# Weight tiles staged a chunk ahead at the changes of operand, and the bias table written in the first stage from GpSimd's queue

## The chip, the cores and the metric

The kernel runs on one core of a Trainium2 chip. What counts is the time of one execution on the device in microseconds. The kernel before took 2283.38, 2283.22 and 2278.28 us in three runs; the median is 2283.22 us.

## What is computed

One decoder layer for a prompt of 2048 tokens and for 8 single-token samples, with width 1024. All tokens share the weights, so the kernel works on 2056 columns of tokens:

```python
h = x * (1 + scale) + shift                       # scale, shift, gate from silu(c) @ w_ada + b_ada
u_s, z_s, q, k, v, z_a, g_s, g_a = split(h @ w_in)
b_s = (GLU(gelu(S5(u_s))) * silu(z_s)) @ w_branch_s
b_a = (attention(q, k, v) * silu(z_a)) @ w_branch_a
m   = sigmoid(g_s) * b_s + sigmoid(g_a) * b_a
x   = LayerNorm(alpha * x + gate * (m @ w_out))
```

The attention looks at a window of 128 keys with a bias by distance. The bias is a table of 32 buckets by 16 heads, `rel_bias`. The kernel turns it into a row of 384 numbers for each head and writes that row 128 times into a scratch tensor in device memory, `biasD` (16 heads x 128 x 384 numbers, 3 MB). Read back with a step of 383, it gives the band of biases for a block of queries. The 8 samples use the same table without the scratch tensor.

## The kernel before

**Products.** Every large matrix product goes through `split_w`, `chunk` and `products`. A weight tile of 1024 x 128 numbers is loaded into `wst` (L55, one buffer). ScalarE rounds it to `whi` (L58) and VectorE takes the rest, `wlo` (L59). An operand X lies in five chunks of tokens (512, 512, 512, 256, 264 wide), each as a high and a low part. One chunk of one job is 24 matmuls (L78): 8 slices of the contraction by three terms. `products` asks for the next job's weights after the second chunk of a job.

**Stages.** The first stage computes u_s, then two jobs for z_a with the work on gate beside them, then v (`v_proj`, L665). `v_proj` takes 17 tiles of tokens, each of 24 matmuls, copies each result from `acc` (3 buffers in PSUM) to `vt` and sends it to device memory from ScalarE's queue. `vt` shares a pool of two buffers (tag `ev`) with the results of all jobs before it, z among them. The second stage runs the state-space scan beside jobs, the third the attention beside jobs. The third begins with `attn_setup`, which writes the bias table (L895, on SyncE's queue) and computes the 8 samples' attention: scores, a softmax in `t1s`, then a transpose of `t1s` on TensorE (L940). Its jobs are `raw_job`s, which copy `acc` to `zr` on ScalarE (L586, also tag `ev`) and send it to `zsD` from ScalarE's queue (L587).

**Changes of operand.** In the fourth stage the operand changes three times, from h to the scan's output, then to the attention's output, then to the gated output. `turn` does the last two jobs of one operand chunk by chunk, and loads a chunk of the next operand into the space that each chunk leaves. It first loads a chunk (`load(0)`), then takes the second job's weights (`split_w(jobs[1][0])`), and in the last chunk, after the first of the two jobs, the weights of the job after the turn (`split_w(nxt)`). The chunks come in the order 512, 256, 512, 264, 512 columns (`ORD`).

**What sets the order.** The program is not run in the order in which the code is written. A scheduler takes the recorded instructions with their dependences and decides each engine's order, which is then fixed. Every engine works through its own list in order. SyncE (SP), ScalarE (ACT) and, for a transfer that the code puts there, GpSimd (POOL) issue transfers. Transfers from SP and ACT take their completion counters from one set of eight in turn, so a transfer is issued only when the one eight places before it is done. Transfers from GpSimd's queue have counters of their own.

Of the kernel before, what the change touches and what calls it, by code (L numbers as in the profile page):

```python
# [9 lines left out]
F32 = mybir.dt.float32  # L10
# [11 lines left out]
KT = 8  # L22
ORD = (0, 3, 1, 4, 2)
# [16 lines left out]
class Trunk:  # L40
# [5 lines left out]
        return es.enter_context(self.tc.tile_pool(name=name, bufs=bufs, reuse_waits="tile", **kw))  # L46


    def split_w(self, parts, st=None):

        nc = self.nc
        if st is None:
            st = self.wp.tile([128, KT, 128], F32, name="wst", bufs=1)
        for src, dst in parts:
            nc.sync.dma_start(dst(st), src)  # L55
        hi = self.wp.tile([128, KT, 128], F32R, name="whi")
        lo = self.wp.tile([128, KT, 128], F32R, name="wlo")
        nc.scalar.copy(hi, st)  # L58
        nc.vector.tensor_tensor(lo, st, hi, op=OP.subtract)  # L59
        return hi, lo  # L60
# [3 lines left out]

    def chunk(self, W, X, c, tick=None):

        nc = self.nc
        ps = self.gp.tile([128, 512], F32, name="acc")
        for k in range(KT):
            self.chunk_k(ps, W, X, c, k)  # L70
            if tick is not None and k in (2, 5, 7):
                tick()
        return ps

    def chunk_k(self, ps, W, X, c, k):
        (hi, lo), (xh, xl), n = W, X[c], CH[c][1]
        for i, (w, x) in enumerate(((hi, xh), (hi, xl), (lo, xh))):
            self.nc.tensor.matmul(ps[:, :n], w[:, k, :], x[:, k, :], start=(k == 0 and i == 0), stop=(k == KT - 1 and i == 2))  # L78

    def products(self, jobs, X, nxt=None, tick=None, first=ORD):  # L80

        for i, (parts, evac, begin, end) in enumerate(jobs):
            W = self.nextW if self.nextW is not None else self.split_w(parts)
            self.nextW = None
            if begin:
                begin()
            for ci, c in enumerate(ORD if i else first):
                ps = self.chunk(W, X, c, tick)
                evac(c, ps)
                if ci == 1:  # L90
                    p2 = jobs[i + 1][0] if i + 1 < len(jobs) else nxt
                    if p2 is not None:
                        self.nextW = self.split_w(p2)
            if end:
                end()

# [520 lines left out]
    def phase1(self, ues, up):  # L617
        nc, I = self.nc, self.I
        w = I["w_in"][0]
        with ExitStack() as ses:  # L620
            self.sps = self.pool(ses, "sp1", 2, PSUM)
            with ues, ExitStack() as es:
                self.prp = self.pool(es, "prep")
                side = self.ssm_prep()
                jobs = []
                for m in range(1, 8):
                    b, e, f = self.u_job(up, m)
                    if m == 1:
                        def b(b=b, e=e):
                            b()  # L630
                            e(ORD[0], self.early)
                    jobs.append((self.cols(w, U0 + m * 128), e, b, f))
                self.products(jobs, self.X, self.cols(w, ZA0), self.every(3, side), first=ORD[1:])
                for _ in side:
                    pass
            with ExitStack() as es:
                p = self.pool(es, "p1z", 2)
                side = self.gate(p)
                self.products([self.za_job(m) for m in range(2)], self.X, self.cols(w, ZA0 + 256), self.every(2, side))
                for _ in side:  # L640
                    pass
                self.v_proj(p)
        for nm, src in (("sk", "cache_swa_k"), ("sv", "cache_swa_v")):
            self.tc.keep_in_program_order(
                nc.sync.dma_start(self.O[nm][0, :, 0:127].rearrange("b w g d -> b w (g d)"),
                                  I[src][0, :, 1:128].rearrange("b w g d -> b w (g d)")))
# [233 lines left out]
        for h in range(nh):  # L880
            v.tensor_scalar(t1[:, h, kw], t1[:, h, kw], den[:, h:h + 1], None, op0=OP.mult)

    def attn_setup(self, p, pp):
        nc, I = self.nc, self.I
        oh = p.tile([32, 129], F32, name="oh")
        nc.sync.dma_start(oh, I["c_onehot"])
        rb = p.tile([32, 16], F32, name="rb")
        nc.sync.dma_start(rb, I["rel_bias"])
        pr = pp.tile([16, 129], F32, name="pt", bufs=2)
        nc.tensor.matmul(pr, rb, oh, start=True, stop=True)  # L890
        fr = p.tile([16, 384], F32, name="fr")

        nc.vector.memset(fr, NEG)
        nc.vector.tensor_scalar(fr[:, 127:256], pr, 8.0, None, op0=OP.mult)
        nc.sync.dma_start(self.biasD.rearrange("h (r l) -> h r l", l=384), fr[:, None, :].to_broadcast([16, 128, 384]))  # L895

        rr = p.tile([32, NS, 16], F32, name="rr")
        nc.vector.tensor_copy(rr, rb[:, None, :].to_broadcast([32, NS, 16]))
# [23 lines left out]
        for b in range(NS):  # L922
# [6 lines left out]
            for P in range(2):  # L929
                i = b * 2 + P  # L930
# [186 lines left out]
    def phase3(self, n2, n3, ii):  # L1117
        with ExitStack() as es:
            pp = self.pool(es, "sp3", 2, PSUM)
            with ExitStack() as es2:  # L1120
                p = self.pool(es2, "p3s")
                side = self.attn_setup(p, pp)
                self.products([self.raw_job(i) for i in range(n2, n2 + n3)], self.X, self.raw_parts(n2 + n3),
                              lambda: next(side, None))
                for _ in side:
                    pass
            with ExitStack() as es2:
                p = self.pool(es2, "p3", 2)
                side = self.attn_blocks(p, pp, ii)
                self.products([self.raw_job(i) for i in range(n2 + n3, 22)], self.X, self.raw_parts(22), lambda: next(side, None))  # L1130
                for _ in side:
                    pass

    def turn(self, jobs, X, nxt, src, where):

        new = [None] * 5

        def load(c):
            new[c] = self.load_x(c, src, where[c])

        load(0)
        W = [self.nextW, self.split_w(jobs[1][0])]
        for c in ORD:
            for i, (parts, evac, begin, end) in enumerate(jobs):
                ps = self.chunk(W[i], X, c)
                if c == 2 and i == 0:
                    self.nextW = self.split_w(nxt)
                evac(c, ps)
            if c != 2:
                load({0: 1, 1: 2, 3: 3, 4: 4}[c])  # L1150
        return new
# [53 lines left out]
    def phase4(self):  # L1205
        nc, I = self.nc, self.I
# [11 lines left out]
        X = self.turn([self.raw_job(i) for i in (22, 23)], self.X, self.cols(wg, 0), self.from_y, "BAAAA")  # L1218

        first = (0, 3, 1, 2, 4)  # L1220

        def ahead(job, first=ORD, n=6):

            seq = [(m, c) for m in range(n) for c in (ORD if m else first)]
            seq += [(m, c) for c in ORD for m in range(n, 8)]
            loaded, ready = {}, {}

            def load(i):
                if i < len(seq) and i not in loaded:
                    loaded[i] = job.load(*seq[i])  # L1230

            def prep(i):
                if i < len(seq) and i not in ready:
                    ready[i] = job.prep(*seq[i], loaded[i])

            def evac(m, c, ps):
                i = seq.index((m, c))
                load(i)
                prep(i)
                load(i + 1)  # L1240
                job.fin(m, c, ps, ready[i])
                prep(i + 1)

            return [(self.cols(job.w, m * 128), lambda c, ps, m=m: evac(m, c, ps), None, None) for m in range(8)]
# [21 lines left out]
                nc.sync.dma_start(self.ysD[m][:, o:o + n], sg[:, :n])  # L1266

        jobs = ahead(Glu(), first)
        self.products(jobs[:6], X, jobs[6][0], first=first)
        X2 = self.turn(jobs[6:], X, self.cols(wa, 0), self.from_(self.ozD), "ABAAA")  # L1270

        class BranchA:
# [14 lines left out]
                nc.sync.dma_start(self.paD[m][:, o:o + n], t[:, :n])  # L1287

        jobs = ahead(BranchA())
        self.products(jobs[:6], X2, jobs[6][0])  # L1290
        X3 = self.turn(jobs[6:], X2, self.cols(ws, 0), self.from_(self.ysD), "AABAA")

        class BranchS:
# [18 lines left out]
        jobs = ahead(BranchS(), n=8)  # L1312
# [166 lines left out]
```

## Time and profile before

| | |
|---|---|
| profiled execution | 2283.26 us, its span 2281.5 us |
| median of three runs | 2283.22 us |
| TensorE busy | 2227.6 us, 98% of the span |
| VectorE busy | 1462.5 us, 64% |
| ScalarE busy | 787.5 us, 35% |
| GpSimd busy | 342.4 us, 15% |

The span is the time between the first and the last instruction. The rest of the execution, 1.76 us, lies around it. TensorE's granted clock is shown as a share of full speed: 1.00 is 2.4 GHz and 0.50 is 1.2 GHz.

### The profile page before, as it was taken

The numbers are of one execution on the slowest core, as the hardware profiler recorded it, in microseconds if no ns is written. First come the engines' busy times: TensorE is split into PE (matmuls) and PEld (weight loads), VectorE is DVE, ScalarE is ACT, GpSimd is POOL, SyncE is SP. The second block draws the span as 40 slices with busy tenths as digits, with TensorE's granted clock in tenths as the row PEclk, the third lists the DMA queues.
The fourth block names the chain that finished last, engine by engine and source line by source line (L and its number), as shares of the span: only waits on it lengthen the run. The fifth ranks groups of instructions, "written<-read, shape, count | busy, mean of one in ns | idle before, by whom it ended". The sixth has DMA issues, their size and how long they took to land.

```text
span 2281.5 us, 35066 instructions
## 1 busy us (share of the span) xinstructions
PE 2227.6 (98%) x12571; PEld 1908.1 (84%) x12571; DVE 1462.5 (64%) x3576; ACT 787.5 (35%) x1700; POOL 342.4 (15%) x420
## 2 busy tenths in 40 slices
PE   7999999999999999999999999999979999999997
PEld 5888798888888888788888888888868888888886
DVE  4896219897888883168998888565354124124887
ACT  3411212332111111157777677573233123112100
POOL 1100001111111111000000000014541001232232
PEclk9999999999999999999999999999989999999999
DMA  9344523334434343743334343486347447667431
GB/s 298 103 141 144 181 95 105 116 113 119 126 115 116 118 120 95 141 131 111 111 113 140 113 118 107 108 195 187 107 144 229 125 126 243 185 187 224 148 111 66
DMA packets 387502, 317.98 MB, mean 139 GB/s; under 512 B 89334, under 2 KB 331406, under 8 KB 385743
## 3 DMA queue, kind: packets, MB, share of 16 engines
q1 hardware_dynamic: 349616, 260.28, 40.2%
q10 hardware_dynamic: 37712, 55.47, 7.2%
q8 instruction: 99, 1.62, 0.3%
q14 instruction: 75, 0.61, 0.1%
HBM read 195.24 MB, written 122.63 MB: 139 GB/s over the span
## 4 chain that ended last, share of the span: by engine, by line
PE 81%; DMA 8%; DVE 5%; SPq 2%; issue 2%; ACT 1%; POOL 1%; ACTq 0%; POOLq 0%; DVEq 0%
PE acc L78 59%; PE po L1413 7%; PE ps L1045 3%; PE po L1088 3%; PE pt L1072 2%; DMA z<-zsD 2%; PE acc L665 2%; DMA biasD<-fr 2%; DMA tD<-kt 1%; SPq L178 1%; PE yp L817 1%; PE yp L816 1%; PE xp L784 1%; DVE sg L1265 1%; PE tr L230 0%
## 5 line engine op out<-in xcount | busy, mean ns | idle before, releaser
L78 PE MATMUL acc<-hh,whi 128*128 128x512 f32 (+2 forms) x2000 | 713.7, 357 | 0.0
L78 PE MATMUL acc<-hl,whi 128*128 128x512 f32 (+2 forms) x2000 | 704.7, 352 | 0.0
L78 PE MATMUL acc<-hh,wlo 128*128 128x512 f32 (+2 forms) x2000 | 703.3, 352 | 0.1
L78 PEld LDWEIGHTS acc<-hh,whi 128*128 128x128 f32 x2000 | 377.7, 189 | 49.0 <-issue 1.9
L78 PEld LDWEIGHTS acc<-hl,whi 128*128 128x128 f32 x2000 | 378.0, 189 | 48.4 <-issue 1.9
L78 PEld LDWEIGHTS acc<-hh,wlo 128*128 128x128 f32 x2000 | 377.5, 189 | 48.1 <-issue 1.0
L78 PE MATMUL acc<-xh,whi 128*128 128x512 f32 (+2 forms) x960 | 336.5, 351 | 13.5 <-ACT whi L58 13.5
L78 PE MATMUL acc<-xh,wlo 128*128 128x512 f32 (+2 forms) x960 | 334.4, 349 | 2.8 <-DVE wlo L59 2.8
L78 PE MATMUL acc<-xl,whi 128*128 128x512 f32 (+2 forms) x960 | 335.7, 350 | 0.0
L78 PEld LDWEIGHTS acc<-xh,whi 128*128 128x128 f32 x960 | 182.9, 191 | 38.0 <-ACT whi L58 14.8
L78 PEld LDWEIGHTS acc<-xh,wlo 128*128 128x128 f32 x960 | 182.2, 190 | 26.6 <-DVE wlo L59 3.6
L78 PEld LDWEIGHTS acc<-xl,whi 128*128 128x128 f32 x960 | 182.7, 190 | 23.0
L1059 ACT ACTIVATE t<-t,nm 128x256 f32<-128x256 f32 (+1 forms) x256 | 126.5, 496 | 47.2 <-DVE nm L1049 46.2
L59 DVE TENSOR_TENSOR wlo<-wst,whi 128x1024 fp32r<-128x1024 f32 x74 | 96.6, 1306 | 67.9 <-ACT whi L58 65.4
L1172 DVE TENSOR_TENSOR xl<-xst,xh 128x1024 fp32r<-128x1024 f32 (+2 forms) x84 | 101.2, 1225 | 59.9 <-ACT xh L1171 58.3
L58 ACT CAST whi<-wst 128x1024 fp32r<-128x1024 f32 x74 | 77.5, 1048 | 141.6 <-PE acc L78 120.5
L1099 POOL TENSOR_TENSOR o<-o,z 128x512 f32<-128x512 f32 x32 | 43.4, 1355 | 519.2 <-DVE o L1093 472.5
L1171 ACT CAST xh<-xst 128x1024 fp32r<-128x1024 f32 (+2 forms) x84 | 86.0, 1044 | 98.0 <-DMA xst<-mD 34.0
L1049 DVE CUSTOM_DVE_ANT_0 t<-ps,bias,skb 128x256 f32<-128x256 f32 (+1 forms) x256 | 109.8, 472 | 5.9 <-issue 3.1
L1413 PE MATMUL po<-wol,xh 128*128 128x512 f32 (+1 forms) x272 | 102.8, 378 | 0.8 <-DVE wol L1336 0.8
L1413 PE MATMUL po<-woh,xh 128*128 128x512 f32 (+1 forms) x272 | 102.8, 378 | 0.0
L1413 PE MATMUL po<-woh,xl 128*128 128x512 f32 (+1 forms) x272 | 102.7, 378 | 0.0
(362 smaller groups left out, 3357.6 us busy)
## 6 DMA issues: line engine op xcount, KB each, us to landing
wst<-in_w_in SPq DMA_DIRECT2D x50, 512.0 KB
uD<-u ACTq DMA_DIRECT2D x8, 1088.0 KB
u<-uD SPq DMA_DIRECT2D x32, 272.0 KB
yD<-y ACTq DMA_DIRECT2D x64, 132.0 KB
x<-in_x_prompt SPq DMA_DIRECT2D x16, 512.0 KB
wa<-in_w_ada SPq DMA_DIRECT2D x16, 512.0 KB
qf<-qD SPq DMA_DIRECT2D x32, 256.0 KB
z<-zaP SPq DMA_DIRECT2D x32, 256.0 KB
```

The costliest lines, as they stand in the source:

```text
L58: nc.scalar.copy(hi, st)
L59: nc.vector.tensor_tensor(lo, st, hi, op=OP.subtract)
L78: self.nc.tensor.matmul(ps[:, :n], w[:, k, :], x[:, k, :], start=(k == 0 and i == 0), stop=(k == KT - 1 and i == 2))
L665: nc.tensor.matmul(ps[:mt, :256], x[:, k, ts], w[:, k, :], start=(i == 0), stop=(i == 23))
L1045: nc.tensor.matmul(ps[:, a2, kw], s["q"][e][:, 2 * g + a2], kk[:, g, kw], start=(i == 0), stop=(i == 1))
L1049: v.tensor_tensor_reduce(t1[:, h, kw], ps[:, a2, kw], s["bias"][:, 4 * g + h, b0:b0 + kw.stop], -0.125, nsk[:, hs:hs + 1], OP.add, OP.min, ...
L1059: nc.scalar.activation(t1[:, h, kw], t1[:, h, kw], AF.Exp, bias=nm[:, h:h + 1], scale=-1.0, accum_out=den[:, h:h + 1])
L1072: nc.tensor.transpose(pt[:, a], s["t", g][:, a, h * 128:(h + 1) * 128], self.ident)
L1088: nc.tensor.matmul(pr, s["v"][h][:, g], x.rearrange("p a q -> p (a q)"), start=(h == hs[0] and i == 0), stop=(h == hs[-1] and i == 1))
L1171: nc.scalar.copy(xv(hi[:, k - 1:k + 1]), sv(st))
L1172: nc.vector.tensor_tensor(xv(lo[:, k - 1:k + 1]), sv(st), xv(hi[:, k - 1:k + 1]), op=OP.subtract)
L1413: nc.tensor.matmul(ps[:, :w], X[a][:, k, ts], Wo[h * w // 512][b][:, k, ws], start=(i == 0), stop=(i == 23))
```

## The change

The code does two things.

At the changes of operand, loading a weight tile (`stage_w`) and splitting it (`split_w`) are now two calls. The weights of a turn's second job are loaded in the last job of `products` before the turn, after its third chunk (`staged`), and `turn` splits them ahead of `load(0)`. The weights of the job after the turn are loaded a chunk earlier (`c == 4`) and split where they were. Ahead of the first turn it is the last job beside the attention that loads them.

The bias table moves. `bias_rows` is called in the first stage, between the two z_a jobs and `v_proj`. It loads the two small inputs, does the matmul of the table, fills `fr` and writes `biasD`, now with `nc.gpsimd.dma_start`. `attn_setup` loads the two inputs again for the samples and writes no table.

```diff
+    def stage_w(self, parts, st=None):
         if st is None:
             st = self.wp.tile([128, KT, 128], F32, name="wst", bufs=1)
         for src, dst in parts:
-            nc.sync.dma_start(dst(st), src)
+            self.nc.sync.dma_start(dst(st), src)
+        return st
+
+    def split_w(self, parts, st=None):
+
+        nc = self.nc
+        if parts:
+            st = self.stage_w(parts, st)
...
+                if ci == 2 and staged is not None and i + 1 == len(jobs):
+                    self.staged = self.stage_w(staged)
...
+                self.bias_rows(p, self.sps)
                 self.v_proj(p)
...
+    def bias_rows(self, p, pp):
+
+        nc = self.nc
+        oh, rb = self.bias_in(p)
+        pr = pp.tile([16, 129], F32, name="tr")
+        nc.tensor.matmul(pr, rb, oh, start=True, stop=True)
+        fr = p.tile([16, 384], F32, name="fr", bufs=1)
+
+        nc.vector.memset(fr, NEG)
+        nc.vector.tensor_scalar(fr[:, 127:256], pr, 8.0, None, op0=OP.mult)
+        nc.gpsimd.dma_start(self.biasD.rearrange("h (r l) -> h r l", l=384), fr[:, None, :].to_broadcast([16, 128, 384]))
+
     def attn_setup(self, p, pp):
...
-        nc.sync.dma_start(self.biasD.rearrange("h (r l) -> h r l", l=384), fr[:, None, :].to_broadcast([16, 128, 384]))
+        oh, rb = self.bias_in(p)
...
+        W = [self.nextW, self.split_w(None, self.staged)]
         load(0)
-        W = [self.nextW, self.split_w(jobs[1][0])]
         for c in ORD:
             for i, (parts, evac, begin, end) in enumerate(jobs):
                 ps = self.chunk(W[i], X, c)
+                if c == 4 and i == 0:
+                    st = self.stage_w(nxt)
                 if c == 2 and i == 0:
-                    self.nextW = self.split_w(nxt)
+                    self.nextW = self.split_w(None, st)
                 evac(c, ps)
```

Three places show what the scheduler made of it. The first is SyncE's list at the end of the two z_a jobs, before: `zaP<-z` sends a result of z_a, `out_sk` and `out_sv` copy the caches in device memory, 1 MB each.

```order
L614 DMA gateD<-gr 9x256 x4
L550 DMA zaP_153<-z 128x512
L645 DMA out_sk<-in_cache_swa_k 8x2x16256
L645 DMA out_sv<-in_cache_swa_v 8x2x16256
L550 DMA zaP_153<-z 128x264
L55 DMA wst<-in_w_in 128x8x128
L550 DMA zaP_153<-z 128x512
```

The same place on SyncE now:

```order
L621 DMA gateD<-gr 9x256 x4
L557 DMA zaP_153<-z 128x512
L557 DMA zaP_153<-z 128x264
L653 DMA out_sk<-in_cache_swa_k 8x2x16256
L653 DMA out_sv<-in_cache_swa_v 8x2x16256
L53 DMA wst<-in_w_in 128x8x128
L557 DMA zaP_153<-z 128x512
```

The result of 264 columns now stands ahead of the two copies; the last result of 512 columns stands behind them in both.

The second place is GpSimd's list at the end of the first stage, now (`zas` takes the samples' z_a, `zt` is a tile of zeros for the scan's scratch, `dg` belongs to the scan's first pair of groups):

```order
L556 COPY zas<-z 128x8 x2
L908 DMA biasD<-fr 2048x1x384
L702 MEMSET zt 128x112
L775 TENSOR_TENSOR dg<-ident,dT 16x16 x2
L812 MEMSET S 128x2
```

Before, the same rows stand there without the transfer. In SyncE's list of the second stage, the second load of the scan's input (`u<-uD`) now waits for the end of this transfer, since its tile takes the space of `fr`.

The third place is ScalarE's list at the second change of operand, where the weights of the last job of `w_glu` are split. Before (`zs` and `sg` are sigmoids of the gate and of the product):

```order
L1264 ACTIVATE sg<-acc,bglu 128x264
L1255 ACTIVATE zs<-z 128x512 x2
L58 CAST whi<-wst 128x1024
L1264 ACTIVATE sg<-acc,bglu 128x512 x2
L1255 ACTIVATE zs<-z 128x256 x2
L1264 ACTIVATE sg<-acc,bglu 128x512
L1171 CAST xh_17814<-xst 128x1024 x3
```

And now:

```order
L1284 ACTIVATE sg<-acc,bglu 128x264
L1275 ACTIVATE zs<-z 128x512 x2
L63 CAST whi<-wst 128x1024
L1284 ACTIVATE sg<-acc,bglu 128x512 x2
L1275 ACTIVATE zs<-z 128x256 x2
L1284 ACTIVATE sg<-acc,bglu 128x512
L1191 CAST xh_17818<-xst 128x1024 x3
```

Nothing moved here but the numbers of lines and buffers. From the fourth stage's first instruction to the last, all five engines' lists are the same in this sense.

## Rows read from the trace of the kernel before

**Rows 1.** The page's first part: busy us (share of the span) xinstructions.
```profile
PE 2227.6 (98%) x12571; PEld 1908.1 (84%) x12571; DVE 1462.5 (64%) x3576; ACT 787.5 (35%) x1700; POOL 342.4 (15%) x420
```

**Rows 2.** Waits of PE: who waited for whom, us in total, times, longest.
```profile
PE acc L78 <- ACT whi L58: 13.5, 3, 10.4
...
PE pt L940 <- DVE t1s L881: 5.1, 1, 5.1
PE acc L78 <- DVE wlo L59: 2.8, 1, 2.8
```

**Rows 3.** Chain of waits, 895 to 1000: start us, us, what.
```profile
912.73 36.20 DMA biasD<-fr
...
951.67 0.44 PE pt L940
```

**Rows 4.** Timeline of ACT, 900 to 985: start us, us, instruction, [idle before <-releaser].
```profile
914.17 0.33 ACTq L587 DMA_DIRECT2D zsD<-zr  x1
...
930.41 0.59 ACT L586 COPY zr<-acc 128x512 f32<-128x512 f32 x1 [9.42 <-DMA zsD<-zr]
...
947.87 0.58 ACT L586 COPY zr<-acc 128x512 f32<-128x512 f32 x1 [6.87 <-DMA zsD<-zr]
...
948.92 1.28 ACT L876 ACT_TABLE_LOAD   x1 [0.46 <-DMA biasD<-fr]
```

**Rows 5.** Timeline of DVE, 900 to 985.
```profile
940.31 0.15 DVE L873 TENSOR_TENSOR es<-sk,mxs 128x1 f32<-128x1 f32 x1
```

**Rows 6.** Timeline of PE, 944 to 960.
```profile
953.40 0.63 PE L78 MATMUL acc<-hh,wlo 128*128 128x512 f32 x1
953.83 0.63 PE L78 MATMUL acc<-hh,whi 128*128 128x512 f32 x1
...
956.05 0.40 PE L78 MATMUL acc<-hh,whi 128*128 128x512 f32 x1
956.28 0.40 PE L78 MATMUL acc<-hl,whi 128*128 128x512 f32 x1
```

**Rows 7.** Windows: us, PE PEld DVE ACT POOL busy (x), PEclk, DMA share, GB/s.
```profile
953.00:954.00 1.00, 1.00 (x4) 0.81 (x3) 0.73 (x1) 0.72 (x2) 0.00 (x0) 0.50 0.03 7
...
1679.00:1690.00 11.00, 7.90 (x20) 6.18 (x21) 5.75 (x5) 1.83 (x4) 4.17 (x4) 0.52 0.37 119
1726.00:1734.00 8.00, 6.19 (x15) 4.65 (x16) 4.61 (x6) 3.37 (x6) 2.54 (x2) 0.57 0.70 217
```

**Rows 8.** DMA queues, 918 to 948: packets, MB, share of 16 engines (q1: SP's queue).
```profile
q1 hardware_dynamic: 2071, 2.88, 85.0%
```

**Rows 9.** DMA queues, 934 to 938 (q10: ACT's queue).
```profile
q1 hardware_dynamic: 228, 0.35, 76.4%
q10 hardware_dynamic: 123, 0.23, 17.0%
```

**Rows 10.** Timeline of PE, 283 to 300: the first matmul of v_proj.
```profile
283.66 0.28 PE L665 MATMUL acc<-vh,hh 128*128 128x256 f32 x1
```

**Rows 11.** Timeline of ACT, 270 to 372.
```profile
291.57 0.37 ACT L668 COPY vt<-acc 128x256 f32<-128x256 f32 x1 [6.39 <-DMA zaP<-z]
...
293.80 0.37 ACT L668 COPY vt<-acc 128x256 f32<-128x256 f32 x1 [1.86 <-DMA vD<-vt]
...
298.26 0.37 ACT L668 COPY vt<-acc 128x256 f32<-128x256 f32 x1 [1.91 <-PE acc L665]
...
301.14 0.37 ACT L668 COPY vt<-acc 128x256 f32<-128x256 f32 x1 [2.51 <-PE acc L665]
```

**Rows 12.** Timeline of SP, 262 to 372.
```profile
277.76 0.80 SPq L645 DMA_DIRECT2D out_sk<-in_cache_swa_k  x1
...
279.43 0.39 SPq L550 DMA_DIRECT2D zaP<-z  x1
...
286.57 1.56 SPq L550 DMA_DIRECT2D zaP<-z  x1
...
337.20 0.43 SPq L707 DMA_DIRECT2D u<-uD  x1
```

More of the change, by code (lines that the diff above doesn't have):

```diff
@@ L46, in pool @@
         return es.enter_context(self.tc.tile_pool(name=name, bufs=bufs, reuse_waits="tile", **kw))
-    def split_w(self, parts, st=None):
-        nc = self.nc
+    def stage_w(self, parts, st=None):
         if st is None:
@@ L78, in chunk_k, with products @@
             self.nc.tensor.matmul(ps[:, :n], w[:, k, :], x[:, k, :], start=(k == 0 and i == 0), stop=(k == KT - 1 and i == 2))
-    def products(self, jobs, X, nxt=None, tick=None, first=ORD):
+    def products(self, jobs, X, nxt=None, tick=None, first=ORD, staged=None):
         for i, (parts, evac, begin, end) in enumerate(jobs):
@@ L881, in softmax, with bias_in @@
             v.tensor_scalar(t1[:, h, kw], t1[:, h, kw], den[:, h:h + 1], None, op0=OP.mult)
+    def bias_in(self, p):
+        oh = p.tile([32, 129], F32, name="oh", bufs=1)
+        self.nc.sync.dma_start(oh, self.I["c_onehot"])
+        rb = p.tile([32, 16], F32, name="rb", bufs=1)
+        self.nc.sync.dma_start(rb, self.I["rel_bias"])
+        return oh, rb
+    def bias_rows(self, p, pp):
[7 more added lines that the diff above has]
+        nc.gpsimd.dma_start(self.biasD.rearrange("h (r l) -> h r l", l=384), fr[:, None, :].to_broadcast([16, 128, 384]))
     def attn_setup(self, p, pp):
         nc, I = self.nc, self.I
[L885 to L894, printed above, removed]
-        nc.sync.dma_start(self.biasD.rearrange("h (r l) -> h r l", l=384), fr[:, None, :].to_broadcast([16, 128, 384]))
+        oh, rb = self.bias_in(p)
         rr = p.tile([32, NS, 16], F32, name="rr")
@@ L1129, in phase3 @@
                 side = self.attn_blocks(p, pp, ii)
-                self.products([self.raw_job(i) for i in range(n2 + n3, 22)], self.X, self.raw_parts(22), lambda: next(side, None))
+                self.products([self.raw_job(i) for i in range(n2 + n3, 22)], self.X, self.raw_parts(22), lambda: next(side, None),
+                              staged=self.raw_parts(23))
                 for _ in side:
@@ L1268, in phase4 @@
         jobs = ahead(Glu(), first)
-        self.products(jobs[:6], X, jobs[6][0], first=first)
+        self.products(jobs[:6], X, jobs[6][0], first=first, staged=jobs[7][0])
         X2 = self.turn(jobs[6:], X, self.cols(wa, 0), self.from_(self.ozD), "ABAAA")
@@ L1289, in phase4 @@
         jobs = ahead(BranchA())
-        self.products(jobs[:6], X2, jobs[6][0])
+        self.products(jobs[:6], X2, jobs[6][0], staged=jobs[7][0])
         X3 = self.turn(jobs[6:], X2, self.cols(ws, 0), self.from_(self.ysD), "AABAA")
```

## The prediction

> **What bounds the kernel now.** I read the page's first part first: TensorE is busy 2227.6 of 2281.5 us [rows 1], so an edit pays only where it takes away one of TensorE's waits, of which there can be 53.9 us at most, or a stretch of low clock behind one. Then TensorE's waits by what ended them [rows 2]. Three groups touch the change. Three waits for `whi` make 13.5 us, the longest 10.4 and the other two 3.1, and one wait for `wlo` is 2.8; asked window by window, the 10.4 and the 2.8 lie at the start of the second change of operand and nearly all of the 3.1 at its end [rows 2, 7]. One wait of 5.1 us is for `t1s`, the softmax of the samples. Third, the chain of waits in that stretch [rows 3]: 36.20 us of it are the write of `biasD`, and it ends in TensorE's transpose L940 at 951.67. In between stands ScalarE's exponential (L876), which the write releases [rows 4]. VectorE had the exponential's inputs ready at 940.31 [rows 5], but ScalarE came to it at 948.92 [rows 4]: ahead of it in its list stand two copies of `zr` that waited 9.42 and 6.87 us for earlier writes of `zr`, and a transfer whose completion counter the table's write still held. So the 5.1 us are due to the table's write, which slows ScalarE's own writes: the one issued at 914.17 freed its buffer at 930.41, 16.2 us later [rows 4].
>
> **The weight tiles: nothing.** The code asks for them earlier, but the order does not change. ScalarE's list around the `whi` of the longest wait is the same row by row, and so are the others through the whole fourth stage. The split stands behind the same two `zs`, and its load behind the same transfers. I cost this part at 0, and the waits of 10.4, 2.8 and 3.1 us stay, with the half clock after them (0.52 and 0.57 of full speed in those windows [rows 7]).
>
> **The table out of attn_setup: -7.0 us.** The wait of 5.1 us goes [rows 2]. The exponential can start at about 940.5 [rows 5]; with 1.28 us of table load [rows 4] and VectorE's few short steps `t1s` is there at about 943, and TensorE wants it at 951.7 - 5.1 = 946.6 [rows 2, 3]. So nothing else is late there. With the wait goes a stretch of low clock: the granted clock is 0.50 behind it [rows 7], that is 1.2 of 2.4 GHz, and matmuls of 512 columns start 0.43 us apart (953.40, 953.83) where at full clock it is 0.23 (956.05, 956.28) [rows 6]. The slow stretch runs from 951.7 to a place between 953.8 and 956.1, which the timeline puts at 955.6: 3.9 us at half speed, 1.9 us lost. The sum is 7.0. The 5.1 us are the only wait of TensorE between 905 and 1000, so no more can be won there.
>
> **The table into the first stage: +2.2 us.** The matmul, the fill and the scaling move with it; they are short in both places and cancel. The two small loads stand on SyncE's queue ahead of the load of v's weights, which TensorE needs at the same point: 0. The write itself is 2048 packets. Under it SyncE's queue moved 2071 packets in 30 us [rows 8], 69 per us with a few others among them, so the write takes about 30 us wherever it stands. It now starts when TensorE is through with the z_a jobs, at about 285, and with the other transfers between ends at about 320. In this time TensorE does `v_proj`, whose first matmul is at 283.66 [rows 10]. A tile takes 301.14 - 298.26 = 2.88 us [rows 11], and with three `acc` buffers tile 5 can't start until tile 2 is copied to `vt`: it is due at 283.66 + 4 x 2.88 = 295.2. In before, that copy was at 293.80 and over at 294.2 [rows 11], a margin of 1.0 us. It waits for a buffer of the pool `ev`, which is held by the last z until its transfer, issued at 286.57 [rows 12], has landed.
>
> That transfer will land later. The two 1 MB copies are ahead of it in the queue, and they now follow the z of 264 columns, which is ready only for 279.43, so they go out at 279.43 + 0.39 = 279.8 instead of 277.76 [rows 12]: +2.1. The 0.13 MB that no longer lie between count for -0.9, at the 0.58 MB in 4 us of [rows 9]. That alone makes 293.8 + 1.2 = 295.0, the copy ends at 295.4, and the wait is 0.2 us. The table's packets come on top. The lower bound is none of this; before, ScalarE's queue moved 123 packets (0.23 MB) between 934 and 938 while the write went on beside it at 228 packets in the four microseconds [rows 9], nearly its full rate. The upper bound is the 16.2 us of [rows 4]: landing at 286.57 + 16.2 = 302.8, the wait 8.0 us, and 2 us of low clock after it. I take +2 us, nearer to [rows 9], because on the new queue the write stands before no transfer of SyncE or ScalarE. The wait is then 2.2 us, and I count no clock for it. The first `vt` copy, which waited 6.39 us for the z of 264 columns [rows 11], will come at once, but TensorE did not wait for it.
>
> Behind the transfer on GpSimd's list stand `zt` and `dg`, first needed after `v_proj`, at about 283.7 + 17 x 2.88 = 333: hidden, if GpSimd is through with the transfer in 45 us. The second load of `u` now waits for the write's end; it was issued at 337.20 [rows 12], some 17 us after the end that I expect: 0.
>
> The sum: 2283.26 for the profiled execution (0.04 above the median of 2283.22) - 7.0 + 2.2 = 2278.5 us.
>
> On moving a transfer to another queue, the Trainium skill says (DMA: Bandwidth & Descriptors, "Issuing engines are not separate DMA queues") that all queues run on the same 16 engines and interleave there, so that another queue saves issue time only. That speaks against this part, and [rows 9] agree: while q10 had work, both queues' packets went through the same engines, 76.4% and 17.0% of them. By the same page ("Queues, rings and completion order") an engine goes round its queues packet by packet, so a write of `vt` would wait for one packet of the table at most; by that rule the added 2 us would be well under 1, and the time 2276 to 2277 (rival A below). The 16.2 us of [rows 4] do not fit it for the old queue.
>
> **Rivals.**
>
> A. *The first stage hides the write entirely.* The packets share the engines as in [rows 9], the z lands in time, the wait is at most 0.2. Then 2283.3 - 7.0 = 2276.3. Against it is the margin of 1.0 us, which the shifted copies alone use up.
>
> B. *The write starves the writes of `vt`, and TensorE waits in `v_proj` for longer than it did in attn_setup.* There are two `ev` buffers, so a pair of tiles needs one write's time plus some 0.75 for copy and issue; two tiles take 5.76 us on TensorE. From 5.0 us a write on, `v_proj` goes at the pace of the writes. At 16.2 us [rows 4]: tile 5 waits 8 us as above, tiles 5 and 6 end at about 309, and the next pair of copies comes only at the write's end, about 320: 11 more. With twice 2 us of low clock it is 8 + 11 + 4 - 7.0 = +16, 2299. In between, at 8 us a write, a pair of tiles takes 8.75 us, 3.0 more than now, for some three pairs: 2 + 9 + 2 - 7 = +6, 2289. For it: the same write has done this to the same engine's writes of the same kind. Against it: [rows 9], and that the old queue's transfers may have been late for another reason than the 16 engines, which a queue of GpSimd's own avoids.
>
> C. *The queue of GpSimd feeds the write more slowly.* At half the rate it ends at about 350. Then the second `u`, and all that is behind it on SyncE's queue (z results, the scan's scratch), goes out 13 us late, and the scan's first pairs with it. TensorE's list has the scan's matmuls among the products, so it would wait perhaps 8 of these 13, and 2 of clock: 2278.5 + 10 = 2289. No row shows this queue's rate.
>
> D. *The weight tiles come earlier after all.* Then the waits of 10.4, 2.8 and 3.1 go, 16.3 us, and with them about half of TensorE's busy time in the two slow windows (7.90 + 6.19 us [rows 7]), at most 7: 2278.5 - 23 = 2255. Against it: the lists of all engines.
>
> **How the numbers follow.** The forecast has a chance of 0.47, A 0.26, B 0.16, C 0.07, D 0.04. A measurement of this kernel can tell about 0.3%, 6.8 us, from no change. The forecast, -4.8, lies inside; a tenth of it falls out on the fast side, next to nothing on the slow side, even with low clock after the wait. A, at -7.0, is split by the bound: 0.15 faster and 0.11 within. Faster: 0.15 + 0.05 + 0.04 + 0.03 for a baseline that moves by some us (the runs shown spread over 5) = 0.27. Slower: B without its mildest part, 0.14, most of C, 0.05, and 0.02 for what I don't see, 0.21. The rest, 0.52, is within 0.3%. The range: 2271, A less the spread of the runs, to 2292, which holds the milder half of B, and C; D and B's far end are left out.
>
> **What would show it.** Right: the wait for `t1s` is gone, and the clock is 1.00 around it; the first stage has a single new wait of TensorE in `v_proj`, before its fifth tile, of 0.2 to 5 us, ended by ScalarE's copy of `vt`, which in turn waits for `zaP<-z`; the write's packets stand between 285 and about 325 on a queue of its own; the waits for `whi` and `wlo` in the fourth stage are the old ones. Wrong: several waits of some us in `v_proj` (B), SyncE idle before the second `u` (C), a fourth stage without the 10.4 us (D), or a wait of TensorE in attn_setup for something that the table's write had covered.

## The result and the profile after

The changed kernel takes 2308.9 us, median of 6 runs (2303.1 to 2313.2); before takes 2283.5 beside it, 6 runs (2278.3 to 2287.9). The ratio is 1.0108, with a 95% interval of 1.0095 to 1.0120: slower by 25 us, where 4.8 us faster was forecast, and outside the range. The profiled execution has a span of 2307.6 us, 26.1 longer than the one before.

TensorE's waits, whole span (who waited for whom, us in total, times, longest):

```profile
PE acc L673 <- ACT vt L676: 29.7, 1, 29.7
PE acc L83 <- ACT whi L63: 18.2, 3, 13.2
...
PE acc L83 <- DVE wlo L64: 2.4, 1, 2.4
```

Against [rows 2] the 5.1 us for `t1s` are gone, and there is one new wait in `v_proj` that is longer than everything the change could save. The others stand where they stood; the largest, for `whi`, is 18.2 us in all where it was 13.5, and the first experiment comes back to it. The chain of waits in that stretch (start, us, what) says what it hangs on:

```profile
286.76 37.81 DMA zaP<-z
...
324.67 0.38 ACT vt L676
...
325.10 4.91 PE acc L673 x23
```

One write of a `z`, 256 KB, takes 37.81 us to land. ScalarE's timeline shows the buffer behind it, beside [rows 11]: the first copy comes at once, the second waits for the `z`.

```profile
287.37 0.37 ACT L676 COPY vt<-acc 128x256 f32<-128x256 f32 x1 [1.98 <-POOL zt L702]
...
324.67 0.65 ACT L676 COPY vt<-acc 128x256 f32<-128x256 f32 x2 [36.93 <-DMA zaP<-z]
```

SyncE's timeline, beside [rows 12], shows what was put into its queue ahead of that `z`, and GpSimd's the table:

```profile
279.89 0.79 SPq L653 DMA_DIRECT2D out_sk<-in_cache_swa_k  x1
...
286.17 0.39 SPq L53 DMA_DIRECT2D wst<-in_w_in  x1
286.76 2.01 SPq L557 DMA_DIRECT2D zaP<-z  x1
```

```profile
284.96 1.21 POOL L908 DMA_DIRECT2D biasD<-fr  x1 [5.24 <-DVE fr L907]
```

The next weight tile's load (`wst`, 512 KB) stands directly ahead of the `z`. The DMA queues in the middle of the wait, 300 to 310 (packets, MB, share of 16 engines; q0 is GpSimd's queue, q1 SyncE's, q10 ScalarE's):

```profile
q0 software_dynamic: 209, 0.96, 95.6%
q1 hardware_dynamic: 210, 0.11, 3.5%
q10 hardware_dynamic: 72, 0.07, 1.9%
```

This is the place to read slowly. SyncE's queue gets one packet through for each packet of the table, 210 for 209. But a packet of the table here is 0.96 MB / 209 = 4.6 KB, three rows of the table, and takes an engine 16 x 10 us x 0.956 / 209 = 0.73 us, and a packet of the weight tile is 0.5 KB. The tile's load is 1024 such packets, 64 for each engine; 64 rounds of 0.77 us (16 x 10 / 209) are 49 us, longer than the table's write. By this estimate the `z` behind it cannot land before the table is through. The windows show the clock (us, PE PEld DVE ACT POOL busy, PEclk, DMA share, GB/s):

```profile
300.00:310.00 10.00, 0.00 (x0) 0.00 (x0) 0.00 (x0) 0.00 (x0) 0.00 (x0) 0.50 1.01 114
...
320.00:330.00 10.00, 4.90 (x25) 4.91 (x26) 0.00 (x0) 1.02 (x3) 0.00 (x0) 0.53 0.35 97
330.00:340.00 10.00, 10.00 (x91) 10.00 (x90) 0.00 (x0) 1.49 (x4) 0.00 (x0) 1.00 0.16 54
900.00:1000.00 100.00, 100.00 (x584) 85.77 (x583) 21.09 (x52) 17.75 (x38) 5.64 (x20) 1.00 0.38 113
```

TensorE is back at 325 at the lower level, 1.2 GHz. The 0.53 is the mean of the whole window, the idle part included; taken by the microsecond, the clock is 0.50 from 325 to 329 and 0.78 from 329 to 330. That is 4.3 us of work at half speed, 2.2 us lost. From 900 to 1000 it no longer waits at all. From 300 to 310 the 16 DMA engines are busy all through (1.01) and move 114 GB/s: they are occupied, not idle.

### The profile page after: what moved, and what is told of

Same layout as the page of the kernel before. It is cut to its first block, busy times and chain, and to the rows that moved or that the text cites. A ratio compares the mean times of both kernels' runs of the same rounds, so it can differ in the third digit from the quotient of the medians.

```text
span 2307.6 us, 35069 instructions
## 1 busy us (share of the span) xinstructions
PE 2227.1 (97%) x12571; PEld 1907.1 (83%) x12571; DVE 1464.1 (63%) x3576; ACT 788.1 (34%) x1700; POOL 347.9 (15%) x421
## 4 chain that ended last, share of the span: by engine, by line
PE 84%; DMA 7%; DVE 4%; issue 2%; SPq 1%; ACT 1%; POOL 1%; ACTq 0%; POOLq 0%; DVEq 0%
PE acc L83 62%; PE po L1433 7%; PE ps L1062 3%; PE po L1105 3%; PE pt L1089 2%; DMA zaP<-z 2%; DMA z<-zsD 2%; PE acc L673 2%; PE xp L792 1%; PE yp L825 1%; PE yp L824 1%; DMA xst<-ysD 1%; DMA tD<-kt 1%; SPq L185 1%; DVE sg L1285 0%
## 5 line engine op out<-in xcount | busy, mean ns | idle before, releaser
L83 PE MATMUL acc<-xh,whi 128*128 128x512 f32 (+2 forms) x960 | 336.4, 350 | 19.0 <-ACT whi L63 18.2
L83 PEld LDWEIGHTS acc<-xh,wlo 128*128 128x128 f32 x960 | 182.0, 190 | 26.1 <-DVE wlo L64 3.1
```

## The experiments

Theory 1: the engines take a packet of each queue in turn; the table's are slow, and what counts is how many packets stand ahead in the queue of the transfer that is waited for. Rivals: GpSimd's queue is the fault; beside such a write everything waits for its end; the weight tiles have a part in it.

**The weight tiles alone.** The changed kernel with the table's code of before:

```
-                self.bias_rows(p, self.sps)
...
```

> Only the weight-tile edits of the change; the table stays in attn_setup. Theory 1 (all of the loss is the table's write in v_proj): the lists of all engines are those of the kernel before, so the time is its time, 2283 within 7 us; the wait for t1s of about 5 us is there, none for vt. Rival (the weight tiles have a part in it: the changed kernel's fourth stage showed waits of 13.2 and 2.4 us where before had 10.4 and 2.8): about 5 us more than before, 2288.

2284.5 us, ratio 1.0004 (0.9995 to 1.0014). Its waits:

```profile
PE acc L83 <- ACT whi L63: 16.3, 3, 11.9
...
PE pt L947 <- DVE t1s L888: 6.0, 1, 6.0
```

So this half is worth nothing that these runs can tell. With the old code of the weight tiles the longest wait for `whi` is 10.4 us in before, 11.9 in the run with GpSimd's queue in attn_setup below and 12.3 in the one with 128 partitions there; the changed kernel's 13.2 is for the most part this spread between profiles.

**GpSimd's queue alone, at the old place.**

```
-        nc.sync.dma_start(self.biasD...
+        nc.gpsimd.dma_start(self.biasD...
```

> The kernel before with one edit: the table's write in attn_setup is issued on GpSimd's queue instead of SyncE's. Theory 1 (packet by packet, 0.8 us for each of the table's): a write of zr has 8 packets per engine and lands after 7 us or a little more, as the 7 to 10 us that the copies of zr waited in the kernel before; the weight tile's load ends with the write, in time for the next job; the exponential may still be late. 2277 to 2290. Rival (while GpSimd's queue writes the table other transfers hardly move): two writes of zr are held for the whole write, TensorE waits 15 to 25 us for acc, 2300 to 2310.

2284.4 us, ratio 0.9999 (0.9989 to 1.0009), in theory 1's range. The queue by itself costs nothing there: TensorE waits 4.5 us for `zr` and 1.8 for `t1s`, 6.3 where it was 5.1 before. One part of the expectation missed, as ScalarE's timeline shows:

```profile
912.60 0.33 ACTq L587 DMA_DIRECT2D zsD<-zr  x1
...
919.45 0.33 ACTq L587 DMA_DIRECT2D zsD<-zr  x1
927.91 0.59 ACT L586 COPY zr<-acc 128x512 f32<-128x512 f32 x1 [8.49 <-DMA zsD<-zr]
...
943.75 0.37 ACT L586 COPY zr<-acc 128x256 f32<-128x256 f32 x1 [15.25 <-DMA zsD<-zr]
```

The copies take two buffers in turn, so these two writes of `zr` took 15 and 24 us to land, not 7 or a little more. Of that TensorE felt the 4.5 us here.

**The old queue at the new place.** The same edit the other way, in the changed kernel:

```
-        nc.gpsimd.dma_start(self.biasD...
+        nc.sync.dma_start(self.biasD...
```

> The changed kernel with the table's write (16 partitions, 2048 rows, the first stage) on SyncE's queue instead of GpSimd's. In SyncE's list it stands ahead of the two cache copies, the weight tile's load and the last z_a. Theory 1 (what counts is what stands ahead of the last z_a in its queue and how long the engines need for it): about 30 us of table and 7 of copies stand ahead, so the z_a lands at about 320 as with the other queue, the wait is 25 to 35 us and the time 2303 to 2313. Rival (the fault is GpSimd's queue with its long packets): the z_a lands 15 us or more earlier, the wait is under 15 us, and the time is 2290 or less.

2314.0 us, ratio 1.0129 (1.0114 to 1.0144): no better: TensorE waits 36.3 us, and wait and time are both about 1 us over the range. SyncE's timeline:

```profile
284.33 0.65 SPq L908 DMA_DIRECT2D biasD<-fr  x1
285.04 9.32 SPq L653 DMA_DIRECT2D out_sk<-in_cache_swa_k  x1
294.41 4.57 SPq L653 DMA_DIRECT2D out_sv<-in_cache_swa_v  x1
299.08 4.11 SPq L53 DMA_DIRECT2D wst<-in_w_in  x1
303.29 17.33 SPq L557 DMA_DIRECT2D zaP<-z  x1
```

Issues that take 0.4 to 2.0 us in the changed kernel take 4 to 17 us. The two runs together say that the place is at fault, not GpSimd's queue.

**The last z_a on ScalarE's queue, with no load ahead of it.**

```
-            nc.sync.dma_start(self.zaD[m]...
+            (nc.scalar if m < 2 else nc.sync).dma_start(self.zaD[m]...
```

> The changed kernel, but the writes of z_a for m = 0 and 1 are issued on ScalarE's queue. Theory 1 (an engine takes one packet of each queue in turn; the table's packets of 4.5 KB take 0.8 us each, and the last z_a stands behind 64 packets per engine of the weight tile's load, 64 x 0.8 = 51 us, so it lands when the table's write ends): the z_a, 8 packets per engine with nothing ahead of it, lands after about 7 us, at 294. Each vD behind it (9 packets per engine) then takes some 7 to 9 us, and v_proj goes at the pace of two buffers: the 29.7 us turn into several waits, 8 to 15 us together, and the time falls to 2286 to 2293. Rival (while the table is written, hardly anything else moves whatever stands ahead of it): one wait of about 29 us stays, 2309.

2299.9 us, ratio 1.0066 (1.0052 to 1.0080); the waits for `vt` are 20.9 us. Better, but in neither range. The DMA queues from 304 to 312 show the mechanism in pure form, three queues and as many packets of each:

```profile
q0 software_dynamic: 151, 0.70, 86.4%
q10 hardware_dynamic: 145, 0.26, 9.8%
q1 hardware_dynamic: 151, 0.08, 3.2%
```

ScalarE's timeline:

```profile
290.46 0.33 ACTq L557 DMA_DIRECT2D zaP<-z  x1
...
314.04 0.37 ACT L676 COPY vt<-acc 128x256 f32<-128x256 f32 x1 [22.76 <-DMA zaP<-z]
321.52 0.37 ACT L676 COPY vt<-acc 128x256 f32<-128x256 f32 x1 [7.11 <-DMA vD<-vt]
```

The landing took 23 us, not 7: the queue's first packet came only after 303, some 13 us behind the issue, and then 8 packets per engine took 10 us. That first part I had not in the theory. The `z` was also issued later than in the changed kernel, at 290.46 for 286.76, since ScalarE had waited 4.99 us for the buffer of an earlier `z`.

**The load behind the z_a.** An edge of order places it there; the split comes after `v_proj`:

```
+                with self.tc.issue_after(self.zdma.ins):
+                    st0 = self.stage_w(self.cols(w, ZA0 + 256))
                 self.v_proj(p)
+                with self.tc.issue_after(self.vtlast.ins):
+                    self.nextW = self.split_w(None, st0)
```

(`zdma` is the last write of a `z`, `vtlast` the last copy of `vt`.)

> The changed kernel, with the load of the next weight tile placed behind the last z_a in SyncE's list instead of ahead of it, by an edge of order alone. Theory 1 (64 packets per engine ahead of the z_a, one for each of the table's): with nothing ahead the z_a's 8 packets per engine need about 7 us, or 20 if its first packet comes 13 us after the issue as in the run with z_a on ScalarE's queue; it lands at 294 to 307 instead of 324, and the wait of 29.7 falls to 5 to 20 us in one or more pieces: 2286 to 2301. Rival (what stands ahead is of no account, beside the write everything waits for its end): 2309, one wait of about 29 us.

2305.5 us, ratio 1.0098 (1.0081 to 1.0115). The `z` landed at 300.4 and the waits are 18.5 us, both as expected; the time is 4 us over the range. ScalarE's timeline, then TensorE's:

```profile
287.00 0.33 ACTq L682 DMA_DIRECT2D vD<-vt  x1
300.51 0.37 ACT L680 COPY vt<-acc 128x256 f32<-128x256 f32 x1 [13.54 <-DMA zaP<-z]
300.92 0.33 ACTq L682 DMA_DIRECT2D vD<-vt  x1
309.01 0.37 ACT L680 COPY vt<-acc 128x256 f32<-128x256 f32 x1 [8.12 <-DMA vD<-vt]
322.56 0.37 ACT L680 COPY vt<-acc 128x256 f32<-128x256 f32 x1 [13.18 <-DMA vD<-vt]
```

```profile
300.94 0.58 PE L677 MATMUL acc<-vh,hh 128*128 128x256 f32 x1 [6.26 <-ACT vt L680]
...
309.43 0.58 PE L677 MATMUL acc<-vh,hh 128*128 128x256 f32 x1 [4.00 <-ACT vt L680]
...
322.98 0.58 PE L677 MATMUL acc<-vh,hh 128*128 128x256 f32 x1 [8.27 <-ACT vt L680]
```

Three waits instead of one. They give back 11.2 us. Of these the low clock takes 4.3: by the microsecond, TensorE works 13 us at the lower level between 300 and 328, 6.5 us lost where the changed kernel lost 2.2. Another 4.6 are waits further on: 1.4 for `whi` behind `v_proj`, where this version splits late, and 4.9 for 1.7 for `tt` in the scan.

The rival, that all waits for the end, is refuted for the `z`; the writes of `vt` that follow, 9 packets per engine each, take its place. They take 22 us each to land (287.00 to 309.01, 300.92 to 322.56), the first with nothing ahead of it in ScalarE's queue, where 9 rounds of 0.77 us make 7. So the count of packets gives an estimate of the least that a landing takes, and not the landing itself; what makes up the rest is not shown.

**More buffers.** `vt` gets buffers of its own:

```
-                vt = self.ev.tile([128, 256], F32, name="vt", tag="ev")
+                vt = p.tile([128, 256], F32, name="vt", bufs=17)
```

> The changed kernel, but the copies vt have 17 buffers of their own instead of sharing two with the z. If the write costs time only through the held buffers: TensorE does not wait in v_proj at all, no stretch of low clock follows, and with the 5.1 us wait of attn_setup gone the time is 2274 to 2279. Rival (TensorE is held by something else beside the write, such as the weights of the next z_a job, whose load of 64 packets per engine ends only with the table's write at about 322): v_proj is over at about 333 and the tile is needed then, so even this rival gives no wait here, unless the load lands after 333: 2280 to 2290.

2294.4 us, ratio 1.0043 (1.0028 to 1.0058): neither range of the theory. TensorE still waits 14.9 us. ScalarE's timeline:

```profile
308.97 0.37 ACT L676 COPY vt<-acc 128x256 f32<-128x256 f32 x1 [3.49 <-PE acc L673]
325.84 0.33 ACTq L678 DMA_DIRECT2D vD<-vt  x1
326.21 0.37 ACT L676 COPY vt<-acc 128x256 f32<-128x256 f32 x1 [16.87 <-DMA wst<-in_w_in]
```

With six writes issued, the seventh needs a completion counter that the weight tile's load still holds; ScalarE stands at this issue, and its copies behind it. Five of the six issues before it took 2.17 to 3.98 us each, where 0.33 is usual. The buffers were only the first thing to run out.

**The row on 128 partitions.** Each head's row is made eight times, and each partition writes 16 rows instead of 128. First in the changed kernel:

```
+        rw = p.tile([32, 16, 8], F32, name="rw", bufs=1)
+        nc.vector.tensor_copy(rw, rb[:, :, None].to_broadcast([32, 16, 8]))
-        nc.tensor.matmul(pr, rb, oh, start=True, stop=True)
+        nc.tensor.matmul(pr, rw.rearrange("b h j -> b (h j)"), oh, start=True, stop=True)
-        fr = p.tile([16, 384], F32, name="fr", bufs=1)
+        fr = p.tile([128, 384], F32, name="fr", bufs=1)
...
```

> The changed kernel, but the row of the table is made on 128 partitions (each head eight times) and each partition writes 16 of the rows, instead of 16 partitions that write 128 each; same queue, same place, same bytes. Theory 1 with the pace set by the 16 partitions that are read: the write goes at two to three times the 95 GB/s, is over in 10 to 17 us instead of 36, a packet takes 0.3 to 0.4 us, and the wait for vt falls to 0 to 8 us: 2277 to 2286. Rival (the pace is that of GpSimd's queue or of the bytes in DRAM): 36 us and the wait of 29.7 us stay, 2309.

2286.4 us, ratio 1.0010 (1.0001 to 1.0019): 22.5 us better than the change. The wait is 8.5 us; wait and time are both a little over the range. The queues from 290 to 300:

```profile
q0 software_dynamic: 546, 2.47, 60.4%
q1 hardware_dynamic: 844, 0.52, 16.4%
```

A packet of the same 4.5 KB now takes 16 x 10 x 0.604 / 546 = 0.18 us of an engine, a quarter. (The two queues do not go one for one here, 844 for 546; that is left open.) So the number of partitions that are read sets the pace, not GpSimd's queue and not the memory that is written.

Then the same lines in the kernel before, in attn_setup on SyncE's queue:

> The kernel before (table in attn_setup on SyncE's queue), with the row on 128 partitions as in the last one. If 16 partitions set the pace of the write: it takes 10 to 17 us instead of 36, the exponential comes in time, the wait of 5.1 us for t1s goes and 1.9 us of half clock with it, 2276. Rival (the pace is not that of the partitions): 2283, with the wait of 5.1 us.

2275.2 us, ratio 0.9958 (0.9944 to 0.9972), as expected. The window 900 to 1000:

```profile
900.00:1000.00 100.00, 100.00 (x603) 86.35 (x602) 33.46 (x117) 32.32 (x88) 1.66 (x9) 1.00 0.47 149
```

No wait for `t1s`, and the table did not have to move for it.

**Both repairs at the new place**: the edits of the run with 128 partitions and of the one with the load behind the z_a, together.

> The changed kernel with both repairs in its own place: the row on 128 partitions (the write takes 15 us instead of 36) and the load of the weight tile behind the last z_a. Theory 1: the z_a has nothing ahead of it and a packet of the table beside it takes 0.25 us, so it lands by 293 to 296, the wait for vt is 0 to 4 us instead of 29.7, no long stretch of low clock, and the time is that of the table on 128 partitions in attn_setup (2275) or up to 6 us more: 2274 to 2281. Rival (in v_proj any write of that size costs TensorE 8 us or more, as the run with 128 partitions alone, 2286): 2284 to 2290.

2282.8 us, ratio 1.0003 (0.9993 to 1.0014). The mechanism is as expected, the copy that waited for the `z` is at 295.57 and the waits for `vt` are 2.2 us; the time is 2 us over the range. Of the 7.6 us to the last run, 2.2 are that wait, 1.4 a wait for `whi` behind `v_proj`, where this version splits late, and 2.6 more for `tt` in the scan (3.2 for 0.6). From 1640 to 1760, at the changes of operand, TensorE is busy 2.4 us less (98.46 for 100.86), where the profiles differ among themselves by as much.

**The weight tiles really earlier.** The last run but one (128 partitions, attn_setup), and the second tile's cast ahead of ScalarE's `zs` by edges of order:

```
+                if last and ci == 2:
+                    self.staged = self.split_w(staged)
+                if last and ci >= 2:
+                    with self.tc.issue_after(self.cast.ins):
+                        evac(c, ps)
```

and the same around the cast at the end of the change of operand.

> The kernel before with the row of the table on 128 partitions in attn_setup (the run at 2275) and with the weight tiles of the second and third change of operand really split earlier: the cast to whi is placed, by edges of order alone, ahead of ScalarE's zs of the last chunks of the job before, and the cast at the end of the change ahead of the last zs. If the waits for whi are a matter of the order in ScalarE's list: the waits of 12.3, 2.6, 3.5 and 0.8 us go, and some 4 us of half clock behind them: 2275 - 19 - 4 = 2252, at the least 2262 if the zs that now come later make TensorE wait for acc. Rival (the chain of z loads, zs, sg and writes of ysD sets the pace there, and TensorE would stop a chunk later for want of acc): 2270 to 2276.

2264.3 us, ratio 0.9912 (0.9894 to 0.9929): faster than both kernels. Its waits from 1640 to 1760:

```profile
PE acc L83 <- ACT whi L63: 8.4, 1, 8.4
PE acc L83 <- DVE wlo L64: 1.8, 1, 1.8
```

The 12.3 and 2.6 us at the start of the change are down to 1.8: the cast stands at 1655.42 where it stood at 1670.92. The wait at its end grew from 3.5 to 8.4: there the cast, at 1706.51, still stands behind the gate's `z` (1705.98) and, ahead of that, behind casts of the new operand, one of which waited 2.03 us for its load (1704.22). That is 2 us short of the range. So both casts were placed earlier still:

```
-                if last and ci == 2:
+                if last and ci == 1:
+                    self.nextW = self.split_w(nxt)
                     self.staged = self.split_w(staged)
...
-                if c == 2 and i == 0:
-                    self.nextW = self.split_w(nxt if first else None, None if first else st)
+                if i == 0 and c == (2 if first else 4):
+                    self.nextW = self.split_w(nxt)
```

> The run at 2264 with the casts still earlier: the second tile's cast directly behind the first's, ahead of the zs of the next chunk, and the cast at the end of the change ahead of the gate's z of the next products. If it is a matter of the order in ScalarE's list alone: the waits of 8.4 for whi and 1.8 for wlo that were left go, and some 2 us of half clock behind them, 2250 to 2256. Rival (by then the loads of z and the writes of ysD set the pace): TensorE waits as long a little later, for acc (sg), and the time stays at 2260 to 2268.

2264.1 us, ratio 0.9916 (0.9901 to 0.9931): nothing won. ScalarE's timeline:

```profile
1703.32 1.04 ACT L1190 CAST xh<-xst 128x1024 fp32r<-128x1024 f32 x1 [3.95 <-DMA xst<-ozP]
1704.27 1.04 ACT L63 CAST whi<-wst 128x1024 fp32r<-128x1024 f32 x1
```

The gate's `z` is out of the way, but a cast of the new operand still stands ahead, and waits for its load. The time is the rival's, but not for its reason: TensorE waits 7.0 us for `whi`, not for acc.

## Why the prediction was wrong

**The weight tiles: nothing.** Right: 1.0004, and the order that the scheduler made is the old one.

**The table out of attn_setup: -7.0.** Right: the wait and the low clock are gone, and the run that takes this wait away with the table in its old place (128 partitions) is 9 us faster, -6.4 to -12.8 by its interval. One reading slipped without effect: three copies of `zr` waited ahead of the exponential, not two; the one left out waited 9.63 us (at 940.63).

**The table into the first stage: +2.2.** This step failed. The place was right: TensorE's fifth tile waits for the copy of the second, `vt`, which waits for the last `zaP<-z`. The size was wrong by more than ten times: 29.7 us and 2.2 of clock. "I take +2 us, nearer to [rows 9], because on the new queue the write stands before no transfer of SyncE or ScalarE" does not hold, for two reasons. [rows 9] show two queues with short packets, 0.21 us of an engine for one of the table (16 x 4 x 0.764 / 228) and 0.09 for one of `zr` (16 x 4 x 0.170 / 123); I carried over the share and not the turn. In the turn a transfer lands no sooner than after as many rounds as packets of its own queue stand up to it, and the list put the weight tile's 64 per engine there. And I took the pace of [rows 8], 16 x 30 us x 0.85 / 2071 = 0.20 us for a packet, for GpSimd's queue too. The table's rate there is the same 96 GB/s, but in packets three times as large, and one took 0.73. With 0.20 us, 64 rounds alone are 13 us and a landing near 300, close to the upper bound that I had (302.8) and set aside; the run with 128 partitions at the new place, with 0.18, has its copy at 302.92 and a wait of 8.5 us. With 0.73 the rounds outlast the write. The rule of the Trainium skill (DMA: Bandwidth & Descriptors, "Queues, rings and completion order") that an engine goes round its queues packet by packet agrees with the 209 and 210 packets above; what I drew from it, one packet of delay for a whole transfer, left out the others of the same queue, and the 2276 to 2277 that I gave for it came of that.

**Rival B** had the cause, a starved write, and the direction. The several waits that were to show it did not come, there was one; they came in the run with the load behind the z_a. Its price, 2289 to 2299, was low, since the first transfer to starve was the `z`, for the whole write, and not each `vt` for 16.2 us. Rival C did not happen: the second `u` goes out without a wait. Rival D did not happen either, as the lists had it; its size is borne out in part: a real earlier cast brings 11 us of the 23.

The sum with the measured terms: -7.0 + 29.7 + 2.2 = +24.9, and the medians differ by 25.4.

## What to carry to other kernels

Before a large write is moved beside other work, list what each queue has outstanding there and count the packets ahead of the transfer that somebody waits for: here that count times the time of one turn (64 x 0.77 us) told that the transfer would be held to the end of the write. It is the least that the delay can be, for transfers with 8 or 9 packets per engine took 15 us and more beside the write, and giving the transfer a queue to itself helped only in part. Make the write itself short first; here spreading its source over 128 partitions gave the gain that the move was to bring, without moving it. Where a scheduler sets the order, an earlier line in the source is no earlier instruction: compare the lists, and place the instruction by an edge if it must come first.

## What the runs showed of the hardware that I had not expected

A write from 16 partitions goes at 96 GB/s on either queue (2.88 MB in 30 us [rows 8], 0.96 MB in 10 us above), and the same bytes from 128 partitions go faster: 247 GB/s on GpSimd's queue (2.47 MB in 10 us above), and in attn_setup the queue of SyncE moved 2305 packets, 3.23 MB with a few others among them, in 9 us (914 to 923), 16 x 9 x 0.962 / 2305 = 0.06 us of an engine for each packet, where it was 0.20 before.

A transfer issued while the engines are full of GpSimd's long packets can send its first packet late: 13 us for the `z` on ScalarE's queue (issued at 290.46, none before 303), and 13 for a weight tile in the run with GpSimd's queue in attn_setup (920.22, none before 933). Why is not settled; no run takes it apart. The issue itself can take long too: 2.17 to 3.98 us for ScalarE's writes of `vt` in the run with 17 buffers, 4 to 17 us on SyncE's queue behind the table.

In `v_proj` the copies of `vt` are 2.72 us apart in some stretches at full clock (332.88 and 335.60 in the changed kernel) and 2.88 in [rows 11]. That is not explained either.
